# Low parts of the normalised input made on GpSimd ahead of the feed-forward products, and constant parameters computed later, in a two-layer hybrid block

## Chip, core and metric

One core of one Trainium2 chip runs the whole program in one launch. The metric is the device time in microseconds (us). The kernel before takes 1329.93 us, the median of three runs (1329.14 to 1330.31). Engines are named as in the profile: PE is TensorE (PEld its weight loads), DVE is VectorE, ACT is ScalarE, POOL is GpSimd, SP issues the DMAs.

## The reference

Two layers, each a mixer (retention, a gated linear recurrence and differential attention on one projection of the input) and a convolutional feed-forward, with an RMS norm ahead of each. 16 meta tokens and 256 tokens of width 1024, all in fp32. The part that the change touches:

```python
def _rms(x):
    xf = x.astype(F32)
    return xf * lax.rsqrt(jnp.mean(xf * xf, axis=-1, keepdims=True) + EPS)

def rms_norm(x, g):
    return (_rms(x) * g.astype(F32)).astype(x.dtype)

def conv_ffn(hn, w_ffn_in, conv_w, conv_b, w_ffn_out, valid):
    l = hn.shape[1]
    u = jnp.where(valid[None, :, None], hn @ w_ffn_in, 0.0)
    up = jnp.pad(u, ((0, 0), (CONV_W - 1, 0), (0, 0)))
    c = conv_b + sum(conv_w[j] * up[:, j:j + l] for j in range(CONV_W))
    gate, val = jnp.split(c, 2, axis=-1)
    return (jax.nn.silu(gate) * val) @ w_ffn_out
...
    lb_soft = jax.nn.softmax(hg_lb.astype(F32), axis=0)
    lbs = jnp.cumsum(lb_soft, axis=0) - lb_soft[0]
    for li in range(DEPTH):
        lambda_init = 0.8 - 0.6 * math.exp(-0.3 * li)
        h = h + mixer(rms_norm(h, norm_mix_g[li]), w_in[li], w_branch[li], w_out[li], lbs[li],
                      da_lambda[li], da_subln_g[li], lambda_init, valid, pos)
        h = h + conv_ffn(rms_norm(h, norm_ffn_g[li]), w_ffn_in[li], ffn_conv_w[li], ffn_conv_b[li],
                         w_ffn_out[li], valid)
```

## The kernel before

**Layout.** Features lie on the 128 partitions, the 272 tokens along the free dimension; `h`, the residual, is 8 tiles of 128x272. In the second layer most outputs are needed for 258 tokens only.

**Products.** A weight matrix is split into tiles of 128x128. Each fp32 operand is the sum of a high part, rounded to the fp32r type, and a low part, and each tile product is three matmuls: high x high (L862), low x high weight (L863), high x low weight (L864). ScalarE makes the high part with a copy into fp32r, and VectorE the low part by subtracting it. For weights that is done for a chunk of 8 tiles at once (`whi`, `wlo` from `wraw`, L583 to L586); one chunk serves 24 matmuls. For x the parts are `xh` and `xl`. A product (one step of the list `ORDER`, two output tiles) takes two chunks, runs over 8 input tiles k, two matmul groups for each, and writes one of two PSUM buffers `main`.

**The norm.** The mean of squares needs all of `h`, and TensorE does not wait for it: class `Norm` first makes `xh` and `xl` from `h` times gain (`take`, L779), without the factor `rstd`, and the first four products are multiplied by `rstd` when they are taken out of PSUM (`evacuate`, L874; in the feed-forward the tile is `two_a`). At the fifth product (`DEFER` = 4) `next` (L811) makes folded parts: GpSimd makes `y` = `h` x `rstd` for the 8 tiles, ScalarE `xh` = `y` x gain rounded, VectorE `xl` = `y` x gain - `xh` in one instruction. Folded tiles 0 to 3 have buffers of their own; folded tiles 4 to 7 lie in the buffers of the unfolded ones, so they can be written only when the fourth product has read those.

**The feed-forward.** The products `fi` 0 to 21 give two tiles each (gate and value). The first four are called fi0 to fi3 here, and fi4 is the first on folded parts. Behind each product: `two_a` (VectorE, out of PSUM), two ScalarE steps (`two_b` = weight x `two_a` + bias), four VectorE steps of the convolution (`two_b<-two_a,small,two_b`), a Silu on ScalarE, a product on VectorE (`two_b<-two_b`), then the high part `ghi` on ScalarE and the low part `glo` on VectorE for the next matrix.

**Constant parameters.** `parameters()` (L734) makes the softmax of `hg_lb` and the factors of the attention: two exponentials on ScalarE on at most 16 columns, and some twenty small VectorE instructions. The first that needs them is `hg_heads`, whose first instructions (`he<-he,keep,floor`) run from 68.67 us.

**What sets the order.** Nothing runs in program order. `_Plan` records every operation with an engine, an estimated cost and a due time (`plan.key`), then orders all engines' queues by a list schedule on these estimates (`order`, L407) and issues the result. Each engine works strictly through its queue and waits by semaphores. Estimates are in `_Engine` (L518); for GpSimd they are 0.04 us + 0.85 ns for each element of a partition, plus 1.6 ns for anything but a memset. A ScalarE function of another table set costs a table load, which the planner prices as well. The recorded operations all carry L549, so they are told apart by their tiles.

Of the kernel before, what the change touches and what calls it, by code (L numbers as in the profile page):

```python
# [11 lines left out]
F32 = mybir.dt.float32  # L12
F32R = mybir.dt.float32r
U8 = mybir.dt.uint8
AF = mybir.ActivationFunctionType
ALU = mybir.AluOpType
PSUM = bass.MemoryType.PSUM
ADD, SUB, MUL = ALU.add, ALU.subtract, ALU.mult
# [7 lines left out]
KD = D // P  # L26
# [14 lines left out]
EARLY = 12.0  # L41
# [182 lines left out]
def _constants():  # L224
# [36 lines left out]
    def even(keys, queries):  # L261
# [12 lines left out]
S_GM, S_GF, S_LB, S_SUB, S_CW, S_CB, S_LAM, S_END = np.cumsum(  # L274
    [0, DEPTH * KD, DEPTH * KD, DEPTH * 8, DEPTH, DEPTH * 3 * 2 * FK, DEPTH * 2 * FK,
     DEPTH * 4 * DA_DH]).tolist()
# [241 lines left out]
class _Engine:  # L518
# [5 lines left out]
    def __getattr__(self, method):  # L524
        f = getattr(self.engine, method)

        def call(*args, **kw):
            aps = [(k, x) for k, x in list(enumerate(args)) + list(kw.items()) if isinstance(x, bass.AP)]
            outs = [x for k, x in aps if k in (0, "out", "accum_out")]
            ins = [x for k, x in aps if k not in (0, "out", "accum_out")]  # L530
            n = math.prod(outs[0].shape[1:])
            cost = self.fixed + self.each * n
            if self.name == "act":
                cost += 0.093 * (len(aps) - 2) - (0.043 if ins[0].tensor.name in self.plan.psum else 0.0)
            elif self.name == "pool" and method != "memset":
                cost += 1.6e-3 * n
            if method == "reciprocal":
                cost += 7 * self.each * n
            elif method == "tensor_tensor_scan":
                cost += self.each * n  # L540
            elif method == "transpose":
                cost = 0.11
            elif method == "matmul" and args[1].dtype == F32R:
                cost = max(0.107, n / 2400 + 0.003)
            elif method == "matmul":
                cost = max(0.214 if args[1].shape[-1] > 32 else 0.07, 4 * n / 2400)
            elif method == "dma_start":
                cost = self.fixed + self.each * n * outs[0].shape[0]
            self.plan.add(self.name, lambda: f(*args, **kw), cost, outs, ins, args[2] if method == "activation" else None)  # L549

        return call
# [56 lines left out]
def _trace(ctx, tc, plan, a, depth, probe):  # L608
    nc = tc.nc
    act = _Engine(plan, nc.scalar, "act", 0.094, 0.833e-3)  # L610
    dve = _Engine(plan, nc.vector, "dve", 0.068, 1.042e-3)
    pe = _Engine(plan, nc.tensor, "pe", 0.0, 4 / 2400)
    pool = _Engine(plan, nc.gpsimd, "pool", 0.04, 0.85e-3)
# [45 lines left out]
    def stt(out, x, s, y, op0, op1):  # L659
        dve.scalar_tensor_tensor(out=out, in0=x, scalar=s, in1=y, op0=op0, op1=op1)  # L660
# [12 lines left out]
    small = fixed([P, S_END], "small")  # L673
# [94 lines left out]
    class Norm:  # L768

        def __init__(self, g, first=0, adds=dve):
            self.g, self.first, self.adds = g, first, adds
            self.acc = temp2("sum", 1)[:, :, first:]
            self.rest = None
            self.folded = False
            self.pairs = 0
# [33 lines left out]
        def next(self):  # L811

            self.pairs += 1
            if self.pairs != DEFER + 1:
                return
            self.folded = True
            ys = []
            for k in range(KD):
                plan.key = clock[0] - 12.0 + 0.3 * k
                if k % 4 == 0:  # L820
                    ys.append(slot4("y"))
                y = ys[-1][:, k % 4, :]
                pool.tensor_tensor(out=y, in0=h[:, k, :], in1=rstd, op=MUL)
                plan.key = clock[0] - 6.0 + 0.7 * k
                hi, lo = x_tile(k, True)
                act.activation(hi, y, AF.Identity, scale=self.g[:, k : k + 1])
                stt(lo, y, self.g[:, k : k + 1], hi.bitcast(F32), MUL, SUB)

    def le_set():

# [106 lines left out]
    for li in range(depth):  # L937
# [5 lines left out]
        if li == 0:  # L943
            norm = Norm(small[:, S_GM : S_GM + KD], adds=pool)
            for k in range(KD):
                plan.key = 1.4 * k - 4.0
                norm.take([k])
            for j in range(4):
                plan.key = 1.0 + 2.5 * j
                norm.square([2 * j, 2 * j + 1])  # L950
            norm.finish()
            plan.key = 13.0 + EARLY
            parameters()
        st = {}

# [440 lines left out]
        for name, j in ORDER:  # L1396
# [18 lines left out]
            elif name[0] == "*":  # L1415
                plan.key = clock[0] - MARGIN
                n = name[1:]
# [10 lines left out]
            if name in BASE:  # L1428
                lo = 0 if name in FULL else t0
# [55 lines left out]
            elif name in ("b0", "b1", "b2"):  # L1485
                ps = products(st["x" + name], name, j, t0)
                g = st["m" + name[1]][:, both, t0:]
                yy = block(f"y{j // 2}")[:, two, t0:]
                if name == "b0":
                    tt(yy, ps, g, MUL)  # L1490
                else:
                    tt(g, ps, g, MUL)
                    tt(yy, yy, g, ADD)
                    if name == "b2":
                        if j == 0:
                            st["yhi"] = [slot4("yhi", F32R) for _ in range(2)]
                            st["ylo"] = [slot4("ylo", F32R) for _ in range(2)]
                        split(st["yhi"][j // 2][:, two, t0:], st["ylo"][j // 2][:, two, t0:], yy)
            elif name == "wo":
                hi, lo = st["yhi"], st["ylo"]  # L1500
                ps = products(lambda k: (hi[k // 4][:, k % 4, :], lo[k // 4][:, k % 4, :]), name, j, t0)
                tt(h[:, both, t0:], h[:, both, t0:], ps, ADD)
                if j == 0:
                    norm = Norm(small[:, S_GF + li * KD : S_GF + (li + 1) * KD])
                norm.take([2 * j, 2 * j + 1])
                norm.square([2 * j, 2 * j + 1])
                if j == 3:
                    norm.finish()
            elif name == "fi":
                ps = products(lambda k: x_tile(k, norm.folded), name, j, t0)  # L1510
                if j % 4 == 0:
                    st.setdefault("ghi", []).append(slot4("ghi", F32R))
                    st.setdefault("glo", []).append(slot4("glo", F32R))
                u = ps
                if not norm.folded:
                    u = temp2("two_a")[:, :, t0:]
                    evacuate(u, ps)
                first = META if last else 0
                c = temp2("two_b")
                for f in range(2):  # L1520
                    ft = j + f * FK
                    w = lambda i: small[:, S_CW + (li * 3 + i) * 2 * FK + ft : S_CW + (li * 3 + i) * 2 * FK + ft + 1]
                    bias = small[:, S_CB + li * 2 * FK + ft : S_CB + li * 2 * FK + ft + 1]
                    act.activation(c[:, f, first:], u[:, f, first - t0 :], AF.Identity, bias=bias, scale=w(2))
                    for back in (1, 2):
                        at = max(first, back)
                        stt(c[:, f, at:], u[:, f, at - back - t0 : T - back - t0], w(2 - back), c[:, f, at:], MUL, ADD)
                c = c[:, :, first:]
                act.activation(c[:, 0, :], c[:, 0, :], AF.Silu)
                tt(c[:, 0, :], c[:, 0, :], c[:, 1, :], MUL)  # L1530
                split(st["ghi"][j // 4][:, j % 4, first:], st["glo"][j // 4][:, j % 4, first:], c[:, 0, :])
            elif last:
                if j == 0:
                    final()
            else:
                hi, lo = st["ghi"], st["glo"]
                ps = products(lambda k: (hi[k // 4][:, k % 4, :], lo[k // 4][:, k % 4, :]), name, j)
                if j == 0:
                    norm = Norm(small[:, S_GM + (li + 1) * KD : S_GM + (li + 2) * KD])
                    le_set()  # L1540
                for ks, x in ([([6], ps[0].unsqueeze(1)), ([7], ps[1].unsqueeze(1))] if j == 3 else [([2 * j, 2 * j + 1], ps)]):
                    if ks[0] == 6:
                        plan.key -= 22 * 0.35
                    if ks[0] == 7:
                        norm.rest = True
                        norm.mean()
                        plan.key = clock[0] - 1.0
                    hk = h[:, ks[0] : ks[-1] + 1, :]
                    tt(hk, hk, x, ADD)
                    norm.square(ks)  # L1550
                    norm.take(ks)
# [20 lines left out]
```

## Time and profile before

| | |
|---|---|
| runs before, median of 3 | 1329.93 us |
| the profiled execution: its time | 1330.22 us |
| its span, first to last instruction | 1328.4 us |
| granted TensorE clock, mean | 0.999 |
| GpSimd, instructions | 161 |
| weights read, `wraw`, 512 KB each | 402 transfers |

The profile is of one execution. Busy shares count an instruction from its start to its end; matmuls overlap, so TensorE's busy time says where it had nothing to do, not how fast it was. A timeline row gives start, duration, engine, line, operation, tiles, shape and count; in brackets stands how long the engine was idle before it and what released it. Rows of equal instructions that follow each other are merged, with their count. A row of the waits gives the total, the number and the longest.

### The profile page before, as it was taken

Reading aid. Unit: us, or ns where it says so; the run is one execution under the profiler, and the core shown is the slowest. Engines: PE = TensorE matmul, PEld = TensorE weight load, DVE = VectorE, ACT = ScalarE, POOL = GpSimd, SP = SyncE. Lnnn points to the kernel's source line nnn. Section 1 sums busy time; section 2 is a strip of 40 time slices with the busy share of each in tenths; the row PEclk is TensorE's granted clock in tenths of the full one; section 3 lists DMA queues with packets and bytes.
Section 4 is the critical chain, followed back from the end, with each engine's and each line's share of the span. In section 5 each row is a group of like instructions: output and inputs, shape, how many; then the busy total and the mean of one; then the engine's idle time right before and its main releaser. Section 6 shows DMA issues by size and latency. Waiting matters only on the chain.

```text
span 1328.4 us, 28916 instructions
## 1 busy us (share of the span) xinstructions
PE 1317.2 (99%) x11862; PEld 1288.8 (97%) x11862; DVE 962.0 (72%) x1630; ACT 813.3 (61%) x1372; POOL 83.6 (6%) x161
## 2 busy tenths in 40 slices
PE   9999999999999999999999999999999999999998
PEld 9999999999999999999999999999999999999986
DVE  7575777697576689886564757776985867898753
ACT  6747454746676567665446474557565775766643
POOL 5000000001010020000030000000011100200000
PEclk9999999999999999999999999999999999999999
DMA  7644543443544545555555445444445445465653
GB/s 270 193 142 153 167 161 128 143 143 128 179 139 159 175 159 175 182 170 187 177 173 179 158 157 163 160 136 144 141 153 175 141 160 198 138 208 189 199 184 109
DMA packets 60755, 219.07 MB, mean 165 GB/s; under 512 B 6864, under 2 KB 6992, under 8 KB 60624
## 3 DMA queue, kind: packets, MB, share of 16 engines
q1 hardware_dynamic: 60336, 216.71, 49.6%
q8 instruction: 93, 1.52, 0.5%
q10 hardware_dynamic: 288, 0.52, 0.1%
q14 instruction: 38, 0.31, 0.1%
HBM read 216.16 MB, written 1.05 MB: 164 GB/s over the span
## 4 chain that ended last, share of the span: by engine, by line
PE 94%; DVE 4%; issue 1%; ACT 0%; DMA 0%; SPq 0%; DVEq 0%
PE main L862 27%; PE main L864 27%; PE main L863 26%; PE fo L1372 2%; PE fo L1374 2%; PE fo L1373 2%; PE lev L1053 1%; DVE two_b L549 1%; PE ds L1237 1%; DVE wlo L549 1%; PE ms L549 1%; PE do L549 1%; PE ro L549 1%; PE ho L549 1%; PE vt L549 1%
## 5 line engine op out<-in xcount | busy, mean ns | idle before, releaser
L862 PE MATMUL main<-xh,whi 128*128 128x272 f32 (+1 forms) x2368 | 693.4, 293 | 0.3 <-issue 0.3
L864 PE MATMUL main<-xh,wlo 128*128 128x272 f32 (+1 forms) x2368 | 680.4, 287 | 0.7 <-DVE wlo L549 0.6
L863 PE MATMUL main<-xl,whi 128*128 128x272 f32 (+1 forms) x2368 | 671.7, 284 | 2.8 <-DVE xl L549 2.8
L549 DVE TENSOR_TENSOR wlo<-wraw,whi 128x1024 fp32r<-128x1024 f32 (+1 forms) x408 | 496.8, 1223 | 201.2 <-ACT whi L549 200.3
L549 ACT ACTIVATE whi<-wraw 128x1024 fp32r<-128x1024 f32 (+1 forms) x408 | 426.5, 1048 | 231.5 <-PE main L863 166.1
L863 PEld LDWEIGHTS main<-xl,whi 128*128 128x128 f32 x2368 | 448.9, 190 | 4.0 <-DVE xl L549 3.4
L862 PEld LDWEIGHTS main<-xh,whi 128*128 128x128 f32 x2368 | 445.6, 188 | 2.1 <-issue 0.4
L864 PEld LDWEIGHTS main<-xh,wlo 128*128 128x128 f32 x2368 | 444.6, 188 | 2.0 <-DVE wlo L549 2.0
L549 DVE SCALAR_TENSOR_TENSOR two_b<-main,small,two_b 128x256 f32<-128x256 f32 (+2 forms) x144 | 65.4, 487 | 29.1 <-ACT two_b L549 27.4
L549 ACT ACTIVATE two_b<-main,small 128x272 f32<-128x272 f32 (+1 forms) x72 | 37.3, 566 | 28.7 <-PE main L864 28.7
L549 POOL TENSOR_TENSOR y<-h,rstd 128x272 f32<-128x272 f32 x32 | 34.8, 1121 | 316.4 <-ACT rstd L549 316.4
L864 PE MATMUL main<-ghi,wlo 128*128 128x272 f32 x176 | 51.0, 290 | 0.0
L862 PE MATMUL main<-ghi,whi 128*128 128x272 f32 x176 | 50.9, 289 | 0.0
L863 PE MATMUL main<-glo,whi 128*128 128x272 f32 x176 | 50.2, 285 | 0.0
L549 ACT ACTIVATE vsrc<-main 128x544 f32<-128x544 f32 x24 | 15.0, 626 | 39.4 <-PE main L864 39.2
L862 PE MATMUL main<-b0hi,whi 128*128 128x272 f32 (+1 forms) x128 | 38.2, 298 | 0.0
L862 PE MATMUL main<-b1hi,whi 128*128 128x272 f32 (+1 forms) x128 | 38.1, 298 | 0.0
L864 PE MATMUL main<-yhi,wlo 128*128 128x272 f32 (+1 forms) x128 | 36.7, 286 | 0.0
L864 PE MATMUL main<-b2hi,wlo 128*128 128x272 f32 (+1 forms) x128 | 36.6, 286 | 0.0
L864 PE MATMUL main<-b1hi,wlo 128*128 128x272 f32 (+1 forms) x128 | 36.6, 286 | 0.0
L864 PE MATMUL main<-b0hi,wlo 128*128 128x272 f32 (+1 forms) x128 | 36.6, 286 | 0.0
L862 PE MATMUL main<-yhi,whi 128*128 128x272 f32 (+1 forms) x128 | 36.5, 285 | 0.0
(244 smaller groups left out, 1933.0 us busy)
## 6 DMA issues: line engine op xcount, KB each, us to landing
wraw<-in_w SPq DMA_DIRECT2D x402, 512.0 KB, 3.4
h<-in_h SPq DMA_DIRECT2D x4, 272.0 KB, 5.6
dec<-in_dec SPq DMA_DIRECT2D x2, 544.0 KB, 5.3
wraw<-in_w SPq DMA_DIRECT2D x4, 256.0 KB, 4.9
const<-in_const SPq DMA_DIRECT2D x1, 937.0 KB, 5.9
gain<-in_gl SPq DMA_DIRECT2D x1, 512.0 KB, 5.2
out<-y ACTq DMA_DIRECT2D x2, 256.0 KB, 2.8
out<-y SPq DMA_DIRECT2D x2, 256.0 KB, 2.7
```

The costliest lines, as they stand in the source:

```text
L549: self.plan.add(self.name, lambda: f(*args, **kw), cost, outs, ins, args[2] if method == "activation" else None)
L862: nc.tensor.matmul(o, wh, hi, start=first, stop=False)
L863: nc.tensor.matmul(o, wh, lo, start=False, stop=False)
L864: nc.tensor.matmul(o, wl, hi, start=False, stop=last)
L1053: nc.tensor.matmul(o, keys, x, start=True, stop=True)
L1237: nc.tensor.matmul(ss[m][:, at : at + nk], q[half, hd, q0 : q0 + P], k[half, hd, :nk], start=True, stop=True)
L1372: nc.tensor.matmul(o, gh, wh, start=False, stop=False)
L1373: nc.tensor.matmul(o, gl, wh, start=False, stop=False)
L1374: nc.tensor.matmul(o, gh, wl, start=False, stop=end)
```

## The change

Three edits, and all queues are ordered anew by the planner:

- In the norm of the feed-forward (both layers; `spare=True`), for input tiles 2 to 7, GpSimd also multiplies `y` by the gain in place, ScalarE copies that into `xh` without a factor, and GpSimd subtracts to give `xl`. Tiles 0 and 1, and the norms of the mixer, stay as they were.
- The planner's estimate for a GpSimd instruction on two tensors goes from 1.6 to 3.0 ns for each element.
- `parameters()` is due at 45 us + `EARLY` instead of 13 us + `EARLY`.

```diff
@@ class _Engine
             elif self.name == "pool" and method != "memset":
-                cost += 1.6e-3 * n
+                cost += (3.0e-3 if method == "tensor_tensor" else 1.6e-3) * n
@@ class Norm
-        def __init__(self, g, first=0, adds=dve):
-            self.g, self.first, self.adds = g, first, adds
+        def __init__(self, g, first=0, adds=dve, spare=False):
+            self.g, self.first, self.adds, self.spare = g, first, adds, spare
@@ Norm.next
                 hi, lo = x_tile(k, True)
-                act.activation(hi, y, AF.Identity, scale=self.g[:, k : k + 1])
-                stt(lo, y, self.g[:, k : k + 1], hi.bitcast(F32), MUL, SUB)
+                gain = self.g[:, k : k + 1]
+                if self.spare and k > 1:
+
+                    pool.tensor_scalar(out=y, in0=y, scalar1=gain, scalar2=None, op0=MUL)
+                    act.activation(hi, y, AF.Copy)
+                    pool.tensor_tensor(out=lo, in0=y, in1=hi.bitcast(F32), op=SUB)
+                else:
+                    act.activation(hi, y, AF.Identity, scale=gain)
+                    stt(lo, y, gain, hi.bitcast(F32), MUL, SUB)
@@ start of the first layer
             norm.finish()
-            plan.key = 13.0 + EARLY
+            plan.key = 45.0 + EARLY
             parameters()
@@ behind the product "wo"
                 if j == 0:
-                    norm = Norm(small[:, S_GF + li * KD : S_GF + (li + 1) * KD])
+                    norm = Norm(small[:, S_GF + li * KD : S_GF + (li + 1) * KD], spare=True)
```

## The prediction

> **What bounds the kernel now.** I read the page's busy table first, then the waits of TensorE, then its timeline at the three longest of them.
>
> ```profile
> span 1328.4 us, 28916 instructions
> PE 1317.2 (99%) x11862; PEld 1288.8 (97%) x11862; DVE 962.0 (72%) x1630; ACT 813.3 (61%) x1372; POOL 83.6 (6%) x161
> PE main L863 <- DVE xl L549: 2.8, 3, 1.5
> ```
>
> TensorE sets the time: it is idle 11.2 us of the span, and its longest named wait is for `xl`, the low part of x, three times. The number of matmuls does not change, so the time can only move by what TensorE waits. The places:
>
> ```profile
> 35.37 0.28 PE L862 MATMUL main<-xh,whi 128*128 128x272 f32 x1
> 36.45 0.39 PE L863 MATMUL main<-xl,whi 128*128 128x272 f32 x1 [0.80 <-DVE xl L549]
> ...
> 504.19 0.29 PE L864 MATMUL main<-xh,wlo 128*128 128x272 f32 x1
> 504.32 0.28 PE L862 MATMUL main<-xh,whi 128*128 128x272 f32 x1
> 505.08 0.39 PE L863 MATMUL main<-xl,whi 128*128 128x272 f32 x1 [0.47 <-DVE xl L549]
> ...
> 1153.13 0.28 PE L862 MATMUL main<-xh,whi 128*128 128x258 f32 x1
> 1153.84 0.28 PE L862 MATMUL main<-xh,whi 128*128 128x258 f32 x1
> 1156.68 0.28 PE L862 MATMUL main<-xh,whi 128*128 128x258 f32 x1
> 1158.44 0.39 PE L863 MATMUL main<-xl,whi 128*128 128x258 f32 x1 [1.49 <-DVE xl L549]
> ```
>
> Matmuls start every 0.12 us (504.19 to 504.32; six in 0.71 between 1153.13 and 1153.84). So the stalls are 1.08, 0.76 and 1.76 less 0.12 each: 0.96, 0.64 and 1.64, together 3.2 us. The last two are at tile 4 of fi4, the first product that takes x with the norm folded in. VectorE makes tiles 4 to 7 in one go at the stall (1157.90 below), so fi4 of layer 1 began four steps of 0.71 earlier, at 1153.84, and needs the low part of tile 6 at 1158.22 and of tile 7 at 1158.93. In layer 0 the same count (step 0.75, tile 4 at 504.32) gives 505.93 and 506.68.
>
> VectorE works through this stage almost without a gap, and GpSimd beside it makes it slower. Its timeline in layer 1, then ScalarE's at the stall and GpSimd's before it (start, us, what, count, idle before):
>
> ```profile
> 1142.36 3.74 DVE L549 SCALAR_TENSOR_TENSOR two_b<-two_a,small,two_b 128x256 f32<-128x256 f32 x4
> 1146.02 0.68 DVE L549 TENSOR_TENSOR two_a<-main,rstd 128x516 f32<-128x516 f32 x1
> 1146.63 1.21 DVE L549 TENSOR_TENSOR wlo<-wraw,whi 128x1024 fp32r<-128x1024 f32 x1
> ...
> 1151.27 0.69 DVE L549 TENSOR_TENSOR two_a<-main,rstd 128x516 f32<-128x516 f32 x1
> 1151.88 0.41 DVE L549 TENSOR_TENSOR glo<-two_b,ghi 128x256 fp32r<-128x256 f32 x1
> 1152.21 0.42 DVE L549 TENSOR_TENSOR two_b<-two_b 128x256 f32<-128x256 f32 x1
> 1152.55 1.22 DVE L549 TENSOR_TENSOR wlo<-wraw,whi 128x1024 fp32r<-128x1024 f32 x1
> 1153.68 0.49 DVE L549 SCALAR_TENSOR_TENSOR xl<-y,small,xh 128x272 fp32r<-128x272 f32 x1
> ...
> 1154.85 1.66 DVE L549 SCALAR_TENSOR_TENSOR two_b<-two_a,small,two_b 128x256 f32<-128x256 f32 x4
> 1156.43 1.21 DVE L549 TENSOR_TENSOR wlo<-wraw,whi 128x1024 fp32r<-128x1024 f32 x1
> 1157.56 0.41 DVE L549 TENSOR_TENSOR two_b<-two_b 128x256 f32<-128x256 f32 x1
> 1157.90 1.73 DVE L549 SCALAR_TENSOR_TENSOR xl<-y,small,xh 128x272 fp32r<-128x272 f32 x4
> ...
> 1156.14 0.42 ACT L549 ACTIVATE two_b<-two_b 128x256 f32<-128x256 f32 x1 [0.30 <-DVE two_b L549]
> 1156.47 0.92 ACT L549 ACTIVATE xh<-y,small 128x272 fp32r<-128x272 f32 x2
> ...
> 1139.85 1.50 POOL L549 TENSOR_TENSOR y<-h,rstd 128x272 f32<-128x272 f32 x2 [62.56 <-ACT rstd L549]
> 1143.95 1.87 POOL L549 TENSOR_TENSOR y<-h,rstd 128x272 f32<-128x272 f32 x2
> ```
>
> One instruction starts up to 0.08 us before the record of the last one ends, so I count from start to start. The same four steps of the convolution (conv) take 3.66 us while GpSimd makes the tiles of `y` (1142.36 to 1146.02), and 1.58 after it (1154.85 to 1156.43): 0.92 against 0.40 each. GpSimd goes from 0.75 to 0.94. Each meeting of a VectorE instruction on two SBUF operands with a GpSimd one costs VectorE 0.5 us.
>
> **The change part by part.** (1) The constant parameters leave the start.
>
> ```profile
> 32.97 0.53 ACT L549 ACTIVATE p<-p 128x16 f32<-128x16 f32 x2 [5.41 <-DVE p L549]
> 33.41 1.05 ACT L549 ACTIVATE whi<-wraw 128x1024 fp32r<-128x1024 f32 x1
> ...
> 58.10 1.05 ACT L549 ACTIVATE whi<-wraw 128x1024 fp32r<-128x1024 f32 x1
> 60.45 1.06 ACT L549 ACTIVATE whi<-wraw 128x1024 fp32r<-128x1024 f32 x1 [1.29 <-PE main L863]
> 63.57 0.63 ACT L549 ACTIVATE hg<-main 128x544 f32<-128x544 f32 x1 [2.06 <-PE main L864]
> 50.68 1.28 ACT L549 ACT_TABLE_LOAD   x1
> ```
>
> Their exponentials hold ScalarE's queue for 5.41 us, and behind them wait a `whi` and the high parts that the stall at 35.37 is for. Without them that queue runs 5 us earlier, tile 4 is in time, and the 0.96 goes. In the built order of the changed kernel they stand between the `whi` of 58.10 and the `hg` of 63.57, with two table loads that are new (Exp, then back to Silu): 2 x 1.28 and 2 x 0.22, 3.0 us, against idle 1.29 + 2.06 = 3.35. Hidden, by 0.3; without that cover up to 3.0 would move the `hg` copy, whose PSUM buffer TensorE wants back one product later. VectorE's part, some twenty small instructions, waits for `whi` in the same gaps. Value: -1.0, between -1.0 and 0.
>
> (2) In both feed-forward norms tiles 2 to 7 lose one VectorE instruction (0.42) and win two on GpSimd: `y` times gain, and the difference. ScalarE's copy stays, without the gain. No DMA is added or moved, SP's queue is the same. The difference is a GpSimd instruction of two operands like `y`: 0.75 alone. The product by a gain is between a copy of 128x128 and `y`:
>
> ```profile
> 174.74 0.36 POOL L549 COPY tw<-rk 128x128 f32<-128x128 f32 x1
> 383.77 0.20 POOL L549 COPY dt<-two_a 128x16 f32<-128x16 f32 x1 [1.02 <-DVE two_a L549]
> 384.38 1.13 POOL L549 COPY dt<-two_a 128x16 f32<-128x16 f32 x1 [0.41 <-DVE two_a L549]
> 384.23 1.22 DVE L549 TENSOR_TENSOR wlo<-wraw,whi 128x1024 fp32r<-128x1024 f32 x1
> ```
>
> I take 0.56 (0.36 plus half of the 0.4 to `y`). The last rows show that a GpSimd copy of one operand, too, waits for a VectorE instruction (1.13 for 0.20), so I let the product meet VectorE like the others.
>
> (3) The new prices of GpSimd make the planner order the queues anew, and this is where I see the loss. The built program of after has, in layer 1 (fi3's convolution is the third from the last):
>
> ```
> ScalarE: ... whi | silu | xh4 xh5 | ghi | conv fi3 x2 | whi | silu fi3 | xh6 | whi | xh7
> GpSimd:  y x8 | gain 2 3 4 5 | lo 2 3 | lo 4 5 | gain 6 7 | lo 6 7
> VectorE: wlo xl0 xl1 mul conv x4 two_a glo mul wlo | conv glo conv x3 wlo mul two_a wlo glo conv x4
> ```
>
> `xh6` stands behind fi3's Silu, which waits for the third of the last four `conv`; it also waits for gain 6, and gain 6 and 7 stand in GpSimd's queue behind `lo 5`, which waits for `xh5`. Before, all four `xh` stood ahead of fi3's evacuation, and the stall ended at 1158.44. Now VectorE without any new meeting: up to the bar its entries are those that run from 1146.63 to 1153.68 in before, so it passes the bar at 1153.68. Then conv 0.40, glo 0.33, three conv 1.18, wlo 1.13, mul 0.34, two_a 0.61, wlo 1.13, glo 0.33, three conv 1.18: 1160.3. Silu 0.4 and xh6 0.4 more, GpSimd's difference 0.8: 1161.9, needed at 1158.22, so 3.7 late. `xh7` stands behind one more `whi`: 1.05 + 0.4 + 0.8 from xh6's end (1161.15) gives 1163.4, needed at 1158.93: 4.5 late. Lateness is not added up: TensorE ends by the largest. Against 1.64 now: +2.9.
>
> Meetings: ten GpSimd instructions (gain 2 to 7, lo 2 to 5) must pass before lo 6. Some fall beside two_a, which reads PSUM, or wait together behind one wlo. Between none and ten I take six of 0.5: +3.0, so 7.5 late, net +5.9. Bounds +2.9 and +7.9.
>
> Layer 0 is the same with another order: xh6 behind fi2's Silu and one whi, xh7 behind fi3's two_a and its two ScalarE steps. Rows:
>
> ```profile
> 493.95 1.21 DVE L549 TENSOR_TENSOR wlo<-wraw,whi 128x1024 fp32r<-128x1024 f32 x1
> 495.85 1.98 DVE L549 SCALAR_TENSOR_TENSOR two_b<-two_a,small,two_b 128x271 f32<-128x271 f32 x4
> ```
>
> In before this wlo stands behind one xl of 0.40 that now follows it, so it starts at 493.55. From there VectorE does wlo, xl, mul, xl, four conv (1.9), wlo, glo, mul, two_a, wlo, glo, three conv: 9.4 us, to 502.9; silu, whi, xh6, lo6 (0.4 + 1.05 + 0.4 + 0.8) to 505.65, in time. Then conv, wlo, mul, two_a (2.5) to 505.5, two ScalarE steps as long as xh (0.5), xh7, lo7: 507.8, needed 506.68: 1.1 late without meetings, 4.1 with six, 6.1 with ten. Against 0.64: +3.5, bounds +0.5 and +5.5.
>
> Sum: -1.0 + 5.9 + 3.5 = +8.4. The profiled execution took 1330.2 (span 1328.4 and 1.8 around it; median of the runs 1329.93), so **1338.6**. Lower bound -1.0 + 2.9 + 0.5: 1332.6. Upper: 0 + 7.9 + 5.5: 1343.6.
>
> **The rivals.**
> A. No new meetings: GpSimd's gains and differences fall where VectorE reads PSUM or waits. For it: GpSimd itself waits for `xh` much of the time, and a gain is shorter than `y`. Against: VectorE's rows above follow each other without a gap. Then only the order of the queues costs: 1332.6.
> B. It is faster: the low parts come ahead of fi4 and all three stalls go. Point of decision: Silu of fi3 done by 1157.0, that is 3.5 us earlier than the sum of VectorE's rows allows. 1330.2 - 3.2 = 1327.0.
> C. The start does not gain: tile 4 waits at 35 us for something else than the exponentials, or the table loads at 60 us stop the `hg` copies. 1339.6.
> D. VectorE waits out a whole GpSimd instruction at each meeting, 0.75 and not 0.5: six times 0.25 in each layer, +3.0: 1341.6. Against it the rows of 0.92 = 0.40 + 0.52. [...]
>
> **How the numbers follow.** Forecast 0.60, A 0.14, B 0.05, C 0.09, D 0.12. A difference under 0.2% (2.7 us) can't be told from none here; A's 1332.6 lies on that edge, half of it counts as same. So faster 0.05, same 0.07, slower 0.88. The range 1332.6 to 1342.6 leaves out B, half of A and the top of D.
>
> **What would show it.** Right: TensorE's wait at 35 us gone; waits for `xl` now released by POOL, at tiles 6 or 7 of fi4, some 4 us in layer 0 and 7 in layer 1; the exponentials near 60 us with no TensorE wait after them; VectorE's conv at 0.9 each beyond the eight `y`. Wrong: waits for `xl` under 1 us in both layers (B), or TensorE waiting on `wlo` or `main` instead.

## The result and the profile after

| | before | after |
|---|---|---|
| median of six runs, us | 1329.88 (1329.14 to 1331.37) | 1338.29 (1337.20 to 1339.22) |
| ratio, 95% interval | | 1.0058 [1.0049, 1.0068] |
| the profiled execution: time, span | 1330.22, 1328.4 | 1339.22, 1337.4 |
| granted TensorE clock, mean | 0.999 | 0.996 |

The change costs 8.4 us. One execution of e5 below (3308.3 us) and one of e8 (2600.0 us) were far longer than all others at a full clock, and the ratios leave them out. The profiled execution of after is the longest of its six, 0.9 us above the median, so what is read from it adds up to 9.0 and not 8.4. The page of the kernel after, its busy line, and TensorE's waits (total, number, longest):

```profile
span 1337.4 us, 28948 instructions
PE 1322.6 (99%) x11862; PEld 1293.4 (97%) x11862; DVE 966.4 (72%) x1618; ACT 816.1 (61%) x1374; POOL 115.4 (9%) x185
...
PE main L871 <- DVE wlo L549: 3.1, 6, 1.6
PE main L869 <- DVE two_b L549: 1.4, 1, 1.4
PE main L869 <- DVE two_a L549: 1.4, 2, 1.2
PE main L870 <- POOL xl L549: 1.1, 2, 0.6
```

The matmul lines are seven further down than before (L869 to L871). The wait for an `xl` is no longer the longest: it is 1.1 us in all, released by GpSimd, and in layer 0 only. TensorE now waits for `wlo` and for its PSUM buffers. VectorE has 12 instructions fewer, yet is busy 4.4 us longer (966.4 against 962.0).

Where the time went is read from one matmul that both kernels have, the mean of squares that follows each layer's products; first the rows of before, then those of after:

```profile
482.54 0.62 PE L549 MATMUL ms<-sum,ones_d 128*128 128x272 f32 x2
671.91 0.62 PE L549 MATMUL ms<-sum,ones_d 128*128 128x272 f32 x2
1136.37 0.62 PE L549 MATMUL ms<-sum,ones_d 128*128 128x272 f32 x2
```
```profile
481.48 0.62 PE L549 MATMUL ms<-sum,ones_d 128*128 128x272 f32 x2
675.69 0.62 PE L549 MATMUL ms<-sum,ones_d 128*128 128x272 f32 x2
1140.20 0.62 PE L549 MATMUL ms<-sum,ones_d 128*128 128x272 f32 x2
```

Ahead of the first feed-forward after is 1.06 us earlier, behind it 3.78 later, ahead of the second 3.83 later, and at the end of the span 9.0. So the start gave 1.06, layer 0's feed-forward cost 4.84 and layer 1's 5.2, in these two executions.

TensorE's timeline of after at fi4 and fi5, layer 0:

```profile
504.01 0.28 PE L869 MATMUL main<-xh,whi 128*128 128x272 f32 x1
504.79 0.39 PE L870 MATMUL main<-xl,whi 128*128 128x272 f32 x1 [0.49 <-POOL xl L549]
...
505.38 0.29 PE L871 MATMUL main<-xh,wlo 128*128 128x272 f32 x1
506.86 0.49 PE L869 MATMUL main<-xh,whi 128*128 128x272 f32 x1 [1.19 <-DVE two_a L549]
...
507.60 0.43 PE L869 MATMUL main<-xh,whi 128*128 128x272 f32 x1
508.62 0.59 PE L870 MATMUL main<-xl,whi 128*128 128x272 f32 x1 [0.59 <-POOL xl L549]
509.01 0.43 PE L871 MATMUL main<-xh,wlo 128*128 128x272 f32 x1
509.24 0.43 PE L869 MATMUL main<-xh,whi 128*128 128x272 f32 x1
```

Three gaps from start to start, less 0.12 each: 0.66, 1.36 and 0.90. The first is at tile 5 of fi4, the third at tile 6. The middle one is the first matmul of fi5, which the planner put ahead of fi4's tile 6; it waits for the PSUM buffer out of which VectorE takes fi3 (`two_a`). And from 506.86 on matmuls start every 0.23 us instead of 0.12: the granted clock is halved (0.50 from 507.00 to 513.83). The windows of after (busy time of PE, PEld, DVE, ACT, POOL, then clock, DMA share, GB/s):

```profile
506.00:510.00 4.00, 2.56 (x10) 2.24 (x11) 4.00 (x6) 2.81 (x5) 3.50 (x3) 0.62 0.68 190
510.00:514.00 4.00, 4.00 (x20) 4.00 (x20) 2.51 (x5) 0.87 (x2) 0.00 (x0) 0.52 0.37 115
514.00:518.00 4.00, 4.00 (x34) 4.00 (x33) 3.01 (x6) 3.13 (x6) 0.00 (x0) 1.00 0.22 88
```

20 matmuls in 4 us at a clock of 0.52, 34 at 1.00. Summed over windows of 0.5 us, time times the missing share of the clock is 3.41 us here and 1.71 in layer 1; before has none in these stages. In layer 1 the gaps are 0.42, 1.88 and 0.79 (`wlo`), 0.36 and 1.58 (PSUM buffers). The 1.88 on TensorE, and GpSimd and VectorE at that time:

```profile
1161.63 0.39 PE L870 MATMUL main<-xl,whi 128*128 128x258 f32 x1
1163.63 0.39 PE L871 MATMUL main<-xh,wlo 128*128 128x258 f32 x1 [1.61 <-DVE wlo L549]
...
1152.28 4.43 POOL L549 TENSOR_SCALAR y<-y,small 128x272 f32<-128x272 f32 x4
1158.65 1.93 POOL L549 TENSOR_TENSOR xl<-y,xh 128x272 fp32r<-128x272 f32 x2 [1.94 <-ACT xh L549]
1160.80 1.69 POOL L549 TENSOR_TENSOR xl<-y,xh 128x272 fp32r<-128x272 f32 x2 [0.21 <-ACT xh L549]
1162.47 4.25 POOL L549 TENSOR_SCALAR y<-y,small 128x272 f32<-128x272 f32 x2
...
1158.94 2.92 DVE L549 SCALAR_TENSOR_TENSOR two_b<-two_a,small,two_b 128x256 f32<-128x256 f32 x3
1161.78 1.79 DVE L549 TENSOR_TENSOR wlo<-wraw,whi 128x1024 fp32r<-128x1024 f32 x1
1163.49 0.41 DVE L549 TENSOR_TENSOR two_b<-two_b 128x256 f32<-128x256 f32 x1
```

While GpSimd makes `lo` 2 to 5, three convolution steps take 2.84 us (0.95 each against 0.40) and the `wlo` that TensorE waits for 1.71 against 1.13. Put down to the four differences, that is 2.2 us of VectorE, 0.56 each; the end of the `wlo` falls beside the next gain.

### The profile page after: what moved, and what is told of

Its sections match the earlier page's. It is cut to its first block, busy times and chain, and to the rows that moved or that the text cites. A ratio compares the mean times of both kernels' runs of the same rounds, so it can differ in the third digit from the quotient of the medians.

```text
span 1337.4 us, 28948 instructions
## 1 busy us (share of the span) xinstructions
PE 1322.6 (99%) x11862; PEld 1293.4 (97%) x11862; DVE 966.4 (72%) x1618; ACT 816.1 (61%) x1374; POOL 115.4 (9%) x185
## 4 chain that ended last, share of the span: by engine, by line
PE 92%; issue 3%; DVE 2%; POOL 2%; DMA 0%; ACT 0%; SPq 0%; POOLq 0%; DVEq 0%; ACTq 0%
PE main L869 27%; PE main L871 27%; PE main L870 26%; PE fo L1379 2%; PE fo L1381 2%; PE fo L1380 2%; PE lev L1060 1%; POOL y L549 1%; PE ds L1244 1%; DVE two_b L549 1%; PE do L549 1%; PE ms L549 1%; PE ro L549 1%; PE ho L549 1%; PE vt L549 1%
## 5 line engine op out<-in xcount | busy, mean ns | idle before, releaser
L869 PE MATMUL main<-xh,whi 128*128 128x272 f32 (+1 forms) x2368 | 695.5, 294 | 3.4 <-DVE two_b L549 1.4
L871 PE MATMUL main<-xh,wlo 128*128 128x272 f32 (+1 forms) x2368 | 682.4, 288 | 3.2 <-DVE wlo L549 3.1
L869 PEld LDWEIGHTS main<-xh,whi 128*128 128x128 f32 x2368 | 447.5, 189 | 5.6 <-DVE two_a L549 1.8
L871 PEld LDWEIGHTS main<-xh,wlo 128*128 128x128 f32 x2368 | 446.7, 189 | 4.7 <-DVE wlo L549 4.7
L871 PE MATMUL main<-ghi,wlo 128*128 128x272 f32 x176 | 51.0, 290 | 0.0
L869 PE MATMUL main<-ghi,whi 128*128 128x272 f32 x176 | 50.9, 289 | 0.0
L549 POOL COPY tails<-vsrc 128x32 f32<-128x32 f32 x32 | 9.6, 313 | 419.2 <-ACT vsrc L549 366.4
L869 PE MATMUL main<-b0hi,whi 128*128 128x272 f32 (+1 forms) x128 | 38.2, 298 | 0.0
L869 PE MATMUL main<-b1hi,whi 128*128 128x272 f32 (+1 forms) x128 | 38.1, 298 | 0.0
L871 PE MATMUL main<-yhi,wlo 128*128 128x272 f32 (+1 forms) x128 | 36.7, 286 | 0.0
L871 PE MATMUL main<-b2hi,wlo 128*128 128x272 f32 (+1 forms) x128 | 36.6, 286 | 0.0
L871 PE MATMUL main<-b1hi,wlo 128*128 128x272 f32 (+1 forms) x128 | 36.6, 286 | 0.0
L871 PE MATMUL main<-b0hi,wlo 128*128 128x272 f32 (+1 forms) x128 | 36.6, 286 | 0.0
```

What stands on the lines that cost most here:

```text
L869: nc.tensor.matmul(o, wh, hi, start=first, stop=False)
L871: nc.tensor.matmul(o, wl, hi, start=False, stop=last)
```

## The experiments

Eleven kernels ran, in three groups (e1 to e4, e5 to e8, e9 to e11), each beside its own runs of before (medians 1330.23, 1330.27, 1330.31), the third on another chip. Ratios are to those.

| run | median, us | ratio to before, 95% interval |
|---|---|---|
| e1 parameters alone | 1329.37 | 0.9993 [0.9984, 1.0002] |
| e2 GpSimd's part alone | 1339.24 | 1.0067 [1.0054, 1.0080] |
| e3 old estimate | 1332.84 | 1.0018 [1.0008, 1.0027] |
| e4 TensorE in order | 1342.10 | 1.0089 [1.0075, 1.0102] |
| e5 gain and difference on 16 columns | 1329.15 | 0.9992 [0.9982, 1.0002] |
| e6 gain on 16 columns | 1334.36 | 1.0031 [1.0021, 1.0041] |
| e7 small matmuls at the gaps | 1336.34 | 1.0045 [1.0032, 1.0058] |
| e8 folded parts due 3 us earlier | 1329.52 | 0.9994 [0.9985, 1.0004] |
| e9 GpSimd's work beside | 1339.08 | 1.0068 [1.0055, 1.0082] |
| e10 only its gains beside | 1330.82 | 1.0008 [0.9999, 1.0017] |
| e11 folded parts due 2 us earlier | 1328.51 | 0.9987 [0.9978, 0.9996] |

**The two edits apart.** e1 is the kernel before with this line:

```diff
-            plan.key = 13.0 + EARLY
+            plan.key = 45.0 + EARLY
```

> The kernel before with the later constant parameters alone. Theory (the start gains what the stall at 35 us cost, and nothing is paid later): TensorE's first matmul of fi0 comes about 1.0 us earlier than before, as in the kernel after (484.22 to 483.17 us), the norms of the feed-forward are as before, time 1329.9 - 1.0 = 1328.9 us. Rival C (the start does not gain by this edit; the 1.0 in the kernel after comes from another order of the queues): 1329.9 us, within 0.3.

e2 is the kernel after with that line undone.

> The kernel after with the constant parameters due as before (13 us). Theory (the two edits add up): 1338.3 + 1.0 = 1339.3 us, with the stall at 35 us back and the two feed-forward norms losing 4.8 and 5.4 us as in the kernel after. Rival (they do not add up, since the queues of the feed-forward depend on where the planner stands after the start): more than 1.5 us away from that, with other waits at fi4 and fi5.

They add up: -0.86 alone, and after gets 0.95 slower without it (1339.24 against 1338.29). The interval of e1 just holds no change; its profile has the stall at 35 us gone and the mean of squares at 481.29. One profile says little about a gain of this size: that of e2 has the mean of squares at 481.90, 0.64 earlier than before without the edit, while the profiles of the eleven kernels with the edit have it 0.3 to 1.8 earlier, 1.2 in the mean. In e2 a stall is back, at another place, and the exponentials don't hold ScalarE there (it is not idle before them): VectorE does fourteen of the small parameter instructions from 38.18 to 39.70, and the `xl` that TensorE waits for stands behind them:

```profile
40.49 0.39 PE L870 MATMUL main<-xl,whi 128*128 128x272 f32 x1 [0.86 <-DVE xl L549]
```

**What the new estimate does.** e3 is the kernel after with GpSimd's estimate as before:

```diff
-                cost += (3.0e-3 if method == "tensor_tensor" else 1.6e-3) * n
+                cost += 1.6e-3 * n
```

> The kernel after with the old estimate for GpSimd's instructions on two tensors (1.6 ns). The instructions are the same, but now the planner believes the low parts to be in time: TensorE's queue keeps fi4 whole and then fi5, and all four xh of tiles 4 to 7 stand ahead of fi3's Silu in layer 1. Theory Q (the loss comes from what the new estimate does to the queues: xh6 and xh7 behind fi3's Silu, and fi5's first matmuls ahead of fi4's last, where they wait for PSUM): TensorE's waits shrink to the low parts of tiles 5 to 7 by 1 to 2 us in each layer, 1333 us (1331.5 to 1335). Theory L (the loss comes from GpSimd's gains and differences being slow and meeting VectorE, whatever the order; the new order was the planner's way to lose less): TensorE waits for xl from GpSimd 4 us or more in each layer, 1338 us or more.

1332.84: the same instructions in other queues are 5.5 us faster, as theory Q had it. TensorE's waits at fi4 are 4.6 us in all, and the half clock lies on 3.41 us of layer 0 only.

e4 is the kernel after with TensorE's groups kept in order:

```diff
             plan.main.append(plan.add("pe", run, cost, [to[i, f]], [wh, wl, hi, lo]))
+            if name == "fi" and j >= DEFER:
+                plan.queue(plan.main[-1], plan.main[-2])
```

> The kernel after, but TensorE's matmul groups from fi4 on keep their order (each queued behind the one before). GpSimd's queue is the same as after's, and ScalarE's in the stage of the norm nearly so. Theory L (the low parts are late, and taking up fi5 first covers part of that): TensorE waits for xl6 and xl7 from GpSimd, about 5 us in layer 0 and 8 us in layer 1, as I had forecast for this order, and the time is above after's: 1341 us or more. Theory R (taking up fi5 first is itself a loss, because its first matmul waits for the PSUM buffer that fi3 still holds while fi4's tiles stand behind it): the waits for the main buffers (two_a 1.36 and 0.36, two_b 1.58 us in after) go, and the time is 2 to 3 us below after's: 1335 to 1336 us.

Theory L: 3.8 us worse than after. TensorE's waits in e4:

```profile
PE main L870 <- POOL xl L549: 4.0, 3, 2.4
PE main L869 <- ACT xh L549: 3.0, 1, 3.0
PE main L871 <- DVE wlo L549: 2.5, 5, 1.6
```

This is the lateness that I had forecast for after: from start to start 3.6 us in layer 0 (4.1 forecast) and 7.5 in layer 1 (7.5 forecast), of which 2.3 there are waits for `wlo`. In after, groups of fi5 run in that time: one ahead of fi4's tile 6 and four ahead of tile 7 in layer 0, nine and eleven in layer 1, 0.36 us each.

**GpSimd's time or the order.** e5 keeps every queue of after, but GpSimd's instructions really cover few columns:

```diff
-                    pool.tensor_scalar(out=y, in0=y, scalar1=gain, scalar2=None, op0=MUL)
+                    def part(run, cost, out, ins):
+                        plan.add("pool", run, cost, [out], ins)
+                    c = slice(0, 16)
+                    part(lambda y=y, gain=gain: nc.gpsimd.tensor_scalar(out=y[:, c], in0=y[:, c], scalar1=gain, scalar2=None, op0=MUL),
+                         0.04 + 2.45e-3 * T, y, [y, gain])
                     act.activation(hi, y, AF.Copy)
-                    pool.tensor_tensor(out=lo, in0=y, in1=hi.bitcast(F32), op=SUB)
+                    part(lambda y=y, hi=hi, lo=lo: nc.gpsimd.tensor_tensor(out=lo[:, c], in0=y[:, c], in1=hi[:, c].bitcast(F32), op=SUB),
+                         0.04 + 3.85e-3 * T, lo, [y, hi])
```

> The kernel after with the same queues on every engine, but GpSimd's products by the gain and its differences really work on 16 of the 272 columns only (the planner still sees the full cost). It leaves out the gain and the difference on the other 256 columns, so xh and xl are incomplete. What goes is GpSimd's time in these instructions and their meetings with VectorE; what stays is the order of the queues. Theory M (the order alone costs 1332.6 as I worked out without meetings, and the rest of the loss is GpSimd's durations and meetings): 1332.6, down to 1331 since GpSimd's own two durations go as well; no half clock. Rival (the order of ScalarE's and GpSimd's queues is nearly all of it): 1336 us or more, with xh6 still 4 us late behind fi3's Silu in layer 1.

In e6 only the first of the two is cut.

> As the run before, but only the products by the gain are cut to 16 columns; the differences are whole. It leaves out the gain on 256 columns. The gains took 1.02 to 1.15 us each in the kernel after where I had put 0.56, and cost VectorE 0.23 for a meeting where I had put 0.5; the differences cost 0.52. If the gains are the larger part (they stand ahead of lo 2 to 5 in GpSimd's queue, and six of them take 8 us in each layer), the time comes to 1334 us or less, near the run with both cut. If the meetings of the differences are, it stays at 1336 to 1338 us.

1329.15: with GpSimd's time cut, and VectorE still relieved of its twelve `xl`, the order costs nothing in sum, less than either theory gave. So the order of after is a loss only together with GpSimd's whole instructions. It is 9.1 us below after, of which the gains make 3.9 (1338.29 to 1334.36) and the differences 5.2. e6 lies just above the border that I had set; gains and differences both count, the differences for more in this sequence of cuts. The order shows in one place of e5, fi6's first matmul in layer 1, which waits 1.42 us for the buffer that fi4 kept too long.

**VectorE slowed, or GpSimd's chain late.** e9 is e1 with all its queues unchanged, and GpSimd's work added for nobody (`aside` is a tile that is not read; `spare` is set as in the change):

```diff
                 stt(lo, y, self.g[:, k : k + 1], hi.bitcast(F32), MUL, SUB)
+                if self.spare and k > 1:
+                    pool.tensor_scalar(out=aside[:, 0, :], in0=y, scalar1=self.g[:, k : k + 1], scalar2=None, op0=MUL)
+                    pool.tensor_tensor(out=aside[:, 1, :], in0=y, in1=hi.bitcast(F32), op=SUB)
```

> The run with the later parameters alone (1329.4 us), with all its queues kept, and GpSimd's six products by the gain and six differences added in each feed-forward norm as work beside: they write a tile that nobody reads, and xh and xl are made as before. So GpSimd's instructions meet VectorE's as in the kernel after, but nothing waits for them. Theory V (the loss in the kernel after is VectorE slowed by the meetings; its wlo, its convolution and its xl come late whoever makes xl): six times 0.23 to 0.35 and six times 0.52 make VectorE 4.5 to 5 us later in each layer, of which TensorE's slack takes some: 1335 us or more, with waits for wlo and xl from VectorE. Theory S (the loss is the low parts' own chain through GpSimd, gain, xh and difference, that ends late): 1330.5 us or less.

e10 adds the first of these two instructions only.

> As the run before, but only the six products by the gain are added in each layer, without the differences. Theory V with 0.23 us for each meeting of a gain (1.5 to 2 VectorE instructions beside each, six of them): VectorE 2 to 2.8 us later in each layer, 1331.5 to 1333.5 us. If gains met like differences (0.5, as I had taken): 4.5 us or more later in each, 1334 us or more. Theory S: 1329.4, no change.

e9 takes 1339.08, 9.7 us more than e1, though nothing waits for what was added; TensorE, VectorE and ScalarE run the same instructions in the same order in both. GpSimd's and VectorE's timelines of e9 in layer 1, and its only long wait there on TensorE:

```profile
1158.62 1.75 POOL L549 TENSOR_TENSOR aside<-y,xh 128x272 f32<-128x272 f32 x2
1160.36 1.13 POOL L549 TENSOR_SCALAR aside<-y,small 128x272 f32<-128x272 f32 x1
1161.46 4.33 POOL L549 TENSOR_TENSOR aside<-y,xh 128x272 f32<-128x272 f32 x4
...
1159.66 2.92 DVE L549 SCALAR_TENSOR_TENSOR two_b<-two_a,small,two_b 128x256 f32<-128x256 f32 x4
1162.50 1.78 DVE L549 TENSOR_TENSOR wlo<-wraw,whi 128x1024 fp32r<-128x1024 f32 x1
1164.20 0.97 DVE L549 TENSOR_TENSOR two_b<-two_b 128x256 f32<-128x256 f32 x1
1165.10 2.23 DVE L549 SCALAR_TENSOR_TENSOR xl<-y,small,xh 128x272 fp32r<-128x272 f32 x4
...
1166.14 0.58 PE L868 MATMUL main<-xl,whi 128*128 128x258 f32 x1 [5.26 <-DVE xl L549]
```

Beside the differences four convolution steps take 2.84 us instead of 1.58, `wlo` 1.70 instead of 1.13, the product 0.90 instead of 0.34: 2.4 us in all. Counted from the stage's mean of squares, the `xl` that TensorE stands for starts 3.7 us later than in e1 (25.22 against 21.53), and TensorE's wait is 3.8 longer. Theory V is shown. The sizes come from VectorE's busy time, in e1, e10 and e9:

```profile
PE 1317.0 (99%) x11862; PEld 1289.0 (97%) x11862; DVE 961.3 (72%) x1630; ACT 816.0 (61%) x1374; POOL 82.8 (6%) x161
```
```profile
PE 1318.4 (99%) x11862; PEld 1290.3 (97%) x11862; DVE 963.9 (72%) x1630; ACT 816.3 (61%) x1374; POOL 98.5 (7%) x173
```
```profile
PE 1320.6 (99%) x11862; PEld 1292.6 (97%) x11862; DVE 970.7 (73%) x1630; ACT 816.8 (61%) x1374; POOL 110.6 (8%) x185
```

Twelve gains add 2.6 us to VectorE (0.22 each), twelve differences 6.8 (0.57 each). To GpSimd they are 1.31 and 1.01 us each, waiting included. The gains alone cost 1.45 us of time, below the 1331.5 to 1333.5 that I expected; the intervals of e1 and e10 overlap, so the size is rough. In the profiled execution of e10 TensorE's longest waits grow by 0.4 (layer 0) and 0.5 (layer 1) only, and the half clock takes 1.7 us of clock in layer 1.

**The half clock.** e7 is the kernel after with small matmuls put ahead of seven places of TensorE's queue:

```diff
+FILL = {(0, 'fi', 4, 5, 0): 1, (0, 'fi', 4, 5, 1): 3, (0, 'fi', 4, 6, 0): 2, (1, 'fi', 4, 4, 0): 1, (1, 'fi', 4, 4, 1): 4, (1, 'fi', 5, 4, 0): 2, (1, 'fi', 5, 7, 1): 3}
...
+                for _ in range(fill):
+                    nc.tensor.matmul(spare, ones_d, ones_d, start=False, stop=False)
                 nc.tensor.matmul(o, wh, hi, start=first, stop=False)
```

> The kernel after with the same queues, and 16 small fp32 matmuls (128x128, 0.43 us each as two records of 0.21, from the 22 records of 4.74 us at the start) put into TensorE's queue ahead of the seven places where it waits at fi4 and fi5, writing columns of the PSUM tile that nobody reads: 2.6 us in layer 0 against 2.9 us of waits, 4.3 in layer 1 against 4.6. Theory G (the granted clock falls because TensorE has gaps there): the clock stays at 1.0 in both stages, and the 3.41 + 1.71 us that the half clock cost, less about 0.8 that lay under the waits themselves, are saved: 1334 us. Rival (the fall has nothing to do with the gaps): the half clock stays, and the time is after's or up to 1 us above: 1338 to 1339.5 us.

The clock stays at 1.00 through both stages of the profiled execution (over the whole span 0.998 to 1.000 in the five runs, 0.995 to 0.997 in after's six), and the ratio falls from 1.0058 to 1.0045, 1.7 us; I expected 4. The gaps were filled only in part. The small matmuls start every 0.11 us there, not every 0.21 as at the start of the span, so they cover half of what I had meant, and the four for the gap of 1.88 come behind that wait, of which 1.81 is left. So TensorE's idle time is what lowers the clock here (0.50 for 6.83 us in layer 0 and 3.41 in layer 1 of after, 1.00 in e7), but not every gap has to go. The rest of the half clock seems to have lain under waits: a TensorE at full speed only comes earlier to a `wlo` that VectorE ends when it ends (2.5 us of such waits are left); no run separates the two. That the fall isn't a matter of the gaps' size alone is seen in e2, which has gaps of 0.67, 1.34 and 1.15 in layer 0 and keeps its clock there:

```profile
510.00:514.00 4.00, 4.00 (x34) 4.00 (x33) 3.03 (x7) 2.03 (x5) 0.00 (x0) 1.00 0.33 114
```

Its layer 0 costs 2.70 us where that of after costs 4.84 with like waits: the difference, 2.1, is the half clock's.

What stands ahead of the fall can be read from the traces. Within one execution all changes of the clock lie whole multiples of 3.413 us apart (in after 501.76, 6.83, 651.95 and 3.41 us, which are 147, 2, 191 and 1 of them). Laid on that grid, one of its stretches holds some 30 matmuls in these stages when TensorE doesn't wait (29 from 513.83 to 517.24 in after, 31 from 1169.18 to 1172.60). The stretch ahead of the half clock in layer 0 of after, both stretches of e2 at the same place, and the emptiest of e7:

```profile
503.58:507.00 3.42, 1.75 (x12) 1.31 (x12) 3.42 (x6) 2.29 (x5) 3.42 (x4) 1.00 0.13 17
```
```profile
503.59:507.01 3.42, 2.03 (x15) 1.59 (x13) 3.42 (x5) 2.13 (x4) 3.42 (x3) 1.00 0.09 32
507.00:510.42 3.42, 2.15 (x15) 1.93 (x16) 3.42 (x5) 2.45 (x5) 2.93 (x3) 1.00 0.73 237
```
```profile
1158.82:1162.24 3.42, 1.84 (x15) 1.63 (x15) 3.42 (x5) 0.87 (x2) 3.42 (x3) 1.00 0.10 32
```

From 490 to 520 and from 1145 to 1180 us of all thirteen kernels each stretch at full clock with 12 matmuls or fewer is followed by the half clock (ten of them), and none with 15 or more is; 13 and 14 do not occur there.

**Versions for speed.** e8 and e11 are e1 with the folded parts of the feed-forward norms due earlier (8.0 in e11, 9.0 in e8):

```diff
-                plan.key = clock[0] - 6.0 + 0.7 * k
+                plan.key = clock[0] - (8.0 if self.early else 6.0) + 0.7 * k
```

> A version for speed: the kernel before with the constant parameters due at 45 us, and the folded xh and xl of the feed-forward norms due 3 us earlier (9 us instead of 6 ahead of the product); no GpSimd work is added. In the built queues the four xl of tiles 4 to 7 stand two wlo earlier. Theory: the stalls at fi4 (0.64 and 1.64 us) go and the start keeps its 0.9: 1330.2 - 0.9 - 2.3 = 1327.0 us. Rival (the low parts push fi2's and fi3's steps back, and TensorE waits for a main buffer or a wlo instead): 1329 us or more.

> The version for speed with the folded parts due 2 us earlier instead of 3. The run with 3 us came to 1329.5 with waits for wlo of 0.61, 0.49 and 0.51 us in layer 1 and 0.62 for xl in layer 0. Theory (VectorE has no room left in layer 1, so that an earlier xl only makes a wlo late): 1329.0 to 1329.7, no better. Rival (3 us was too early and 2 us finds room): 1328 us or less.

e11 is faster than before, 0.9987 with an interval below 1; e8, due another 1 us earlier, gains nothing that can be told from none, as its rival had it. At 1328.51 e11 lies between my theory (1329.0 or more) and the rival (1328 or less), and its interval overlaps those of e1 and e8: that the earlier parts gain anything beside the later parameters is not shown by the times. In e11 no wait for `xl` is left in either layer, and what remains is VectorE's `wlo`, 2.1 us in four waits.

## Why the prediction was right, and where only its sum was

The time forecast was 1338.6, measured 1338.29. The stages came out near the terms of the sum: -1.0 against -1.06 for the start, +3.5 against +4.84 and +5.9 against +5.2 for the layers. But the terms were put together otherwise, and errors cancelled: that the sum came within 0.3 us is luck.

- **The start** was right in its size: e1 and e2. ScalarE's queue gained 2.6 us and not 5 (the `whi` of 33.41 runs at 30.77 in e1, behind a wait for TensorE), which was enough; and e2 stalls by VectorE's part of the parameters, which I had priced at nothing. Neither the exponentials near 60 us nor their table loads (1.28 us each, at 58.34 and 60.91 in after) made TensorE wait.
- **Meetings slow VectorE** was right, and e9 shows that they alone are enough for the whole loss. Their size was off: I took six of 0.5 for each layer, 3.0; it is twelve, six at 0.57 and six at 0.22, 4.7 (3.6 for the ten ahead of `lo` 6 that I had counted). That a gain meets VectorE like a difference was the wrong step there. The gain's own duration, 0.56 by my estimate, is 1.1 us for the first four of layer 1 (4.43) and 2.1 for the last two (4.25), waiting included. And I had read 0.94 us for a `y` that meets VectorE; the eight of that stage take 8.6 us in before, 1.08 each.
- **"6 or 7 of fi4, some 4 us in layer 0 and 7 in layer 1"** failed, and what I had named as a sign of error, TensorE waiting on `wlo` or `main`, is what the trace shows. The lateness was right (e4 has it, 3.6 and 7.5), but I had read the new order of ScalarE, GpSimd and VectorE and not that of TensorE: the planner, with the new estimate, believed `lo` 6 and 7 late and put up to eleven groups of fi5 ahead of them. That hides 3.8 us (e4 against after). Rival A's "only the order of the queues costs" failed too: 1332.6 forecast, 1329.15 in e5, probably for the same reason.
- **The half clock** was in no term: 5.1 us at full count, of which e7 wins back 1.7. With the larger meetings it makes up for the cover that I did not see.
- **Rival D**, VectorE waiting out whole instructions, would be 0.75 for each difference. The runs show 0.57 (6.8 us for twelve, e9 against e10). GpSimd is slowed as well (1.01 us for a difference, waiting included, against the 0.75 of a `y` alone), so the two slow each other, but VectorE does not lose 0.75 in the mean.
- **Rivals B and C** fell with the result and with e1.

So the loss as a ladder of runs: parameters -0.9 (e1), GpSimd's work beside VectorE +9.7 (e9), VectorE relieved of six `xl` in each layer -6.2 (e9 to e3), the queues by the new estimate +5.5 (e3 to after): +8.1, against 8.4 measured. The last two steps change the order of some instructions besides, so they are not free of each other.

## What to carry to other kernels

Work moved to GpSimd was not free for VectorE: count every instruction that will run beside VectorE's two-operand ones, here at 0.57 us for one of two tensors and 0.22 for one of a tensor and a gain, before counting the instruction saved (0.42). A planner's estimate is a part of the kernel: making it more true for one instruction (a difference is priced at 1.09 us instead of 0.71, and takes 1.0 in e9 and 1.2 in after) made this one 5.5 us slower. That the other prices were still wrong, a gain's above all (0.71, and it takes 1.3 in e10 and 1.4 in after), is the likely reason; no run tests it. Read the new order of every queue, TensorE's own above all, and price a stall of TensorE with the clock that it may cost afterwards (3.41 us of clock were missing in layer 0 of after).

## What was not expected of the hardware

In after and e3 the granted clock halves behind gaps of TensorE that are all under 2 us, and stays so for 3.41 us or a multiple (1.71, 3.41 or 5.12 us of clock missing in one stage or both of after, e2, e3, e4, e6, e9 and e10; none in either stage of before, e1, e5, e7, e8 and e11). Like gaps cost it in one run and not in another (layer 0: 0.66, 1.36 and 0.90 in after, 0.67, 1.34 and 1.15 in e2). The grid of 3.413 us goes with that: e2's gaps fall on it so that neither stretch holds fewer than 15 matmuls, while the one ahead of after's half clock holds 12. No gap of after lasted a whole stretch (the longest was 1.88 us), so TensorE need not be idle for one. In these stages the half clock came behind each stretch at full clock with 12 of some 30 matmuls or fewer, and behind none with 15 or more; between 12 and 15 no run here settles where the border lies.
